# Two plain gate/up pairs a layer instead of four, with norm sums behind one begun product and FFN operands made name by name

## The chip, the cores and the metric

The kernel runs on one core of one Trainium2 chip. Times are device microseconds of one execution. The three runs of the kernel before took 1186.43, 1184.93 and 1186.91 us; the median, 1186.43 us, is the number that the change is measured against.

## The reference, cut to what matters

A trunk of two decoder layers over 512 tokens of width 1024, in float32. Layer 0 mixes tokens by three groups of dilated window attention, layer 1 by causal trailing means. Behind each mixer stands a SwiGLU feed-forward network (FFN) with 2816 hidden channels, and every part begins with an RMS norm.

```python
def rmsnorm(x, g):
    y = xf * lax.rsqrt(jnp.mean(xf * xf, axis=-1, keepdims=True) + RMS_EPS)
    return (y * g.astype(jnp.float32)).astype(x.dtype)
...
def swiglu_ffn(h, w_gate_up, w_down):
    gu = h @ w_gate_up
    gate, up = gu[..., :D_FF], gu[..., D_FF:]
    return (jax.nn.silu(gate) * up) @ w_down
...
    for i in range(DEPTH):
        ...
        x = x + swiglu_ffn(rmsnorm(x, ffn_norm[i]), w_ffn_gate_up[i], w_ffn_down[i])
    return rmsnorm(x, final_norm)
```

## The kernel before, in words

Channels lie on the 128 partitions and the 512 tokens along the free axis, so x is eight tiles `X[k]` of 128x512. For precision every operand is split into a high and a low part (`split`, line 91: ScalarE rounds the high part, VectorE subtracts it to get the low part), and each logical matmul is three: high by high, high by low, low by high (lines 329 to 332 and 461 to 463).

**Two ways to multiply.** A *plain* product (class `Product`) contracts all eight channel tiles: 24 matmuls of 512 columns. It can begin on x scaled by the norm's weights alone, before the row of 1/rms is known, since that row multiplies the result per token and is applied by VectorE afterwards (`plain_pair`, line 1093: `gt` and `up` are the product times `row`). A *Strassen pair* (`chained`, line 519) makes two output tiles, gate and up, by seven block products of 12 matmuls with 256 columns each, 84 in all, in place of 48 with 512. Its operands are seven combinations of blocks of the normed x (named "11", "1", "2", "21", "3", "22", "4"), kept in the dict `T` for the whole layer, and they need the finished row. `prepare(k)` (line 1108) makes all names for one channel tile `k`. In `chained` most block products accumulate onto one PSUM tile `alpha` one after another, and between two of them ScalarE copies what stands there so far (`a`, `b`, `c`; lines 535, 543 and 551).

**The FFN** (`ffn`, line 1086). There are 22 gate/up pairs j. The first `NPLAIN` = 4 are plain: their matmuls keep TensorE going while VectorE and ScalarE prepare `T`, one tile after each gate product. The others are Strassen pairs. `PARTS` splits the down projection into four parts: hidden tiles 0 to 1 (plain), 2 to 9 and 10 to 17 (block products), 18 to 21 (plain). The down projection of a part is called FF2 here, so FF2 part 1 is the plain one over the first two hidden tiles; it stands between gate/up pair 3 and pair 4.

**The norm in between.** Each finished `X[k]` is scaled and split (`note`, line 397) and squared on ScalarE, and VectorE adds the squares up in `acc`. `finish` (line 436) sums over channels by small matmuls with a tile of ones (`rstd`, line 411), VectorE scales (`var`, line 414), POOL raises to -1/2 (line 417), TensorE spreads the result over partitions (line 424) and ScalarE copies it to `row` (line 430). To cover that, `begin` starts two plain products ahead of the sums on the tiles that are there already, and a third one stands half ahead of the spread and half behind it.

**What sets the order.** Weights go through rings of buffers (`w` has five, `raw` four); `pump` issues loads and one conversion step after another between products, in the order of the list of weights. A plain tile's low part is made "lean": ScalarE writes minus the high part and a DMA of POOL's queue adds the source to it (line 149). A Strassen pair's weights (`Pair`) are three loads by SP and one adding DMA of POOL (line 173); one of its `raw` tiles is then combined by VectorE (lines 189 and 190), and its tiles are split by ScalarE and VectorE. The list of instructions that each engine then works through, strictly in order, is set when the program is built.

Of the kernel before, what the change touches and what calls it, by code (L numbers as in the profile page):

```python
# [15 lines left out]
P = 128  # L16
S = 512
# [21 lines left out]
K2 = KC // 2  # L39
NPLAIN = 4  # L40
WARM = 5
# [8 lines left out]
APART = 28  # L50
NEAR = 11
OPEN = 2
FIXED = NEAR + OPEN
# [12 lines left out]
def trunk(ctx: ExitStack, tc: tile.TileContext, xT, xN, norms, w_first, w_qk, w_qkp, w_v0, w_v0p, w_v12, w_out, w_outp, w_pair, w_down, w_dblock, w_pin, w_pgrp,  # L66
# [134 lines left out]

    turn = [0]
# [176 lines left out]

    def square(layer, k, engine=None):  # L380
        sq = tmp.tile([P, S], F32, name="sq", bufs=3)
        nc.scalar.activation(sq, X[k], AF.Square)
        if layer in acc:
            (engine or nc.vector).tensor_add(sq, acc[layer], sq)
        acc[layer] = sq

    def scaled(layer, k, hi, lo, on_dve=False):
# [7 lines left out]
        operand[layer, k] = hi, lo  # L395

    def note(layer, k):

        if layer < 4:
            held[layer, k], t = slot("h", open=layer == 2 and k == KC - 1)  # L400
            scaled(layer, k, t[:, 0], t[:, 1])
        square(layer, k)
# [197 lines left out]
    with tc.tile_pool(name="opool", bufs=1) as opool:  # L600
        early = [opool.tile([P, 2, S], F32R, tag=f"o{k}", name="early") for k in range(K2)]
        with tc.tile_pool(name="apool", bufs=1) as apool:
# [285 lines left out]
            def halve(h):  # L888

                if h < 3:  # L890
                    OP2[h] = tuple(apool.tile([P, S], F32R, tag=f"qk{h}{c}", name="oh") for c in range(2))
                else:
                    held["o", h], b = slot("oh", open=h == 3)
                    OP2[h] = b[:, 0], b[:, 1]
# [156 lines left out]

            def residual(m, p):
                x = X[m].rearrange("p (q c r) -> p q c r", c=NT, r=NT)
                nc.vector.tensor_add(x, x, p.rearrange("p (r c q) -> p q c r", r=NT, c=NT))
                note(1, m)

            for m in range(NOUT):
                residual(m, lead.pop(0).add([last]).p)
            for u in range(2):
                one, two = (apool.tile([P, S], F32, tag=tag, name="one") for tag in ("s0", "s12"))  # L1060
                seven(T2, one, two, scratch)
                if u:
                    for k in range(2):
                        give(("s", k))
                for c, p in enumerate((one, two)):
                    residual(NOUT + 2 * u + c, p)
            f = Product(HEADS, heads).add(range(HEADS))
            for key in [key for key in held if key[0] == "o"]:
                give(key)
            residual(KC - 1, f.p)  # L1070

    with tc.tile_pool(name="fpool", bufs=2) as fpool:
# [13 lines left out]
        def ffn(layer, nxt, lead, row):  # L1086
# [3 lines left out]
            def gu():  # L1090
                return lead.pop(0).p if lead else product(op)

            def plain_pair(j, up):
                pg = gu()
                gt = ftile("gt")
                nc.vector.tensor_mul(gt, pg, row)
                prepare(j)
                pu = gu()
                if j == NPLAIN - 1:
                    for k in range(KC):  # L1100
                        give((op, k))
                nc.vector.tensor_mul(up, pu, row)
                nc.scalar.activation(gt, gt, AF.Silu)
                nc.vector.tensor_mul(up, up, gt)

            T = {}

            def prepare(k):


                h, t = normed(op, k, row, Temp(), Temp(), True)
                hq, b22 = h.t.rearrange("p (a b c) -> p a b c", a=2, b=2), h.t[:, 3 * H2:]
                held["t", k, 0], b = slot("tb", apart=True)
                split(b[:, 0].rearrange("p (a c) -> p a c", a=2), b[:, 1].rearrange("p (a c) -> p a c", a=2), hq[:, :, 0])
                T["11", k], T["21", k] = (tuple(b[:, e, i * H2:(i + 1) * H2] for e in range(2)) for i in range(2))
                for i, names in enumerate((("1", "2"), ("3", "4"))):
                    held["t", k, 1 + i], b = slot("tt", apart=True)
                    split(b[:, 0], b[:, 1], t.t[:, i * S:(i + 1) * S])
                    for a, name in enumerate(names):
                        T[name, k] = tuple(b[:, e, a * H2:(a + 1) * H2] for e in range(2))  # L1120
                if k % 2 == 0:
                    held["t", k, 3], T["n"] = slot("tn", apart=True)
                n = tuple(T["n"][:, e, k % 2 * H2:(k % 2 + 1) * H2] for e in range(2))
                split_neg(*n, b22)
                T["22", k] = n
                h.done()
                t.done()

# [45 lines left out]
            def strassen_pair(u, first=None, right=None):  # L1174
# [10 lines left out]
                if first:  # L1185
                    hooks.setdefault(2, []).extend([later(give, ("t", k, 1)) for k in range(K2)] + [first])
                if right:
# [8 lines left out]
            def gate_up(j, ahead):  # L1196
                first, block = next((p[0], p[2]) for p in PARTS if p[0] <= j < p[1])
                u = tmp.tile([P, S], F32, tag="sq", name="u", bufs=3) if block or ahead else ftile("up")
                i, odd = (j - first) // 2, j % 2
                if j < NPLAIN:  # L1200
                    plain_pair(j, u)
                elif block and odd and j == FC - 1:
                    strassen_pair(u, later(operands, i, U["even"]), later(operands_right, i, u))
# [23 lines left out]

            j = 0
            for first, end, block in PARTS:
                while j < min(max(end + block, NPLAIN), FC):  # L1230
                    gate_up(j, block and j == end)
# [30 lines left out]

        lead = begin(2, 1, range(KC - 1))
        row = finish(lead, 1, [KC - 1])
        ffn(0, 2, lead, row)
# [11 lines left out]
        lead = begin(2, 2, range(KC - 2))  # L1277
        row = finish(lead, 2, range(KC - 2, KC))
        Y = {}
# [38 lines left out]
        def mix(g):  # L1318
            if g not in M:
                mixed(g)  # L1320
            for c, f in enumerate(M.pop(g)):
                m = 2 * g + c
                nc.vector.scalar_tensor_tensor(X[m], f.p, nrm[:, 5, m:m + 1], X[m],
                                               op0=OP.mult, op1=OP.add)
                held[3, m], t = slot("n")
                scaled(3, m, t[:, 0], t[:, 1])
            for c in range(2):
                square(3, 2 * g + c)
                give(("y", g, c))

        pool(3)
# [195 lines left out]
```

## Time and profile before

| | us |
|---|---|
| median of three runs | 1186.43 |
| the profiled execution: from the first to the last instruction (its span) | 1184.0 |
| ScalarE (ACT) busy | 721.7 |
| GpSimd (POOL) busy | 171.3 |

The difference between span and time, 2.4 us to the median, lies ahead of the first and behind the last instruction. In the rows of the profile PE is TensorE, DVE is VectorE, ACT is ScalarE; L461 is line 461; `ps<-far,w` names the tile written and the tiles read. A timeline row gives start, duration, engine, line, operation, tiles, shape and, in brackets, how long the engine sat idle before it and what ended that. A row of the windows view gives, for one stretch of time, the busy time of PE, PE's weight loads, DVE, ACT and POOL (with the number of instructions), then the granted clock, the DMA engines' busy share and GB/s. A row of the waits list gives the time waited in all, how often, and the longest wait.

### The profile page before, as it was taken

Reading aid. Unit: us, or ns where it says so; the run is one execution under the profiler, and the core shown is the slowest. Engines: PE = TensorE matmul, PEld = TensorE weight load, DVE = VectorE, ACT = ScalarE, POOL = GpSimd, SP = SyncE. Lnnn points to the kernel's source line nnn. Section 1 sums busy time; section 2 is a strip of 40 time slices with the busy share of each in tenths; the row PEclk is TensorE's granted clock in tenths of the full one; section 3 lists DMA queues with packets and bytes.
Section 4 is the critical chain, followed back from the end, with each engine's and each line's share of the span. In section 5 each row is a group of like instructions: output and inputs, shape, how many; then the busy total and the mean of one; then the engine's idle time right before and its main releaser. Section 6 shows DMA issues by size and latency. Waiting matters only on the chain.

```text
span 1184.0 us, 25180 instructions
## 1 busy us (share of the span) xinstructions
PE 1175.4 (99%) x10042; PEld 1119.9 (95%) x10042; DVE 989.0 (84%) x1733; ACT 721.7 (61%) x1262; POOL 171.3 (14%) x165
## 2 busy tenths in 40 slices
PE   9999999999999999999999999999999999999997
PEld 7889999999999989889999999988889999999997
DVE  7997898889789888699988988656789998898875
ACT  6554564546455557747756775775575766676553
POOL 1101111111111002311111111122130111111100
PEclk9999999999999999999999999999999999999999
DMA  8537667666856557957777877798595777877732
GB/s 302 130 95 187 147 153 166 168 160 152 192 140 169 145 157 195 246 113 203 191 188 189 204 184 209 195 265 208 121 195 119 187 199 195 198 191 193 197 92 72
DMA packets 83766, 207.57 MB, mean 175 GB/s; under 512 B 7856, under 2 KB 13120, under 8 KB 83648
## 3 DMA queue, kind: packets, MB, share of 16 engines
q1 hardware_dynamic: 52672, 144.84, 36.9%
q0 software_dynamic: 30688, 60.83, 31.6%
q8 instruction: 78, 1.28, 0.4%
q14 instruction: 40, 0.33, 0.1%
q10 hardware_dynamic: 288, 0.29, 0.1%
HBM read 203.84 MB, written 2.10 MB: 174 GB/s over the span
## 4 chain that ended last, share of the span: by engine, by line
PE 96%; DMA 1%; issue 1%; DVE 1%; ACT 0%; POOL 0%; POOLq 0%; DVEq 0%; ACTq 0%
PE ps L461 21%; PE ps L462 20%; PE ps L463 20%; PE ps L329 7%; PE ps L330 7%; PE ps L332 7%; PE ps L928 2%; PE ps L632 2%; PE ps L633 2%; PE ps L634 2%; DMA raw<-w_outp 1%; PE ps L847 1%; PE ps L716 1%; PE ps L736 1%; PE ps L841 1%
## 5 line engine op out<-in xcount | busy, mean ns | idle before, releaser
L92 ACT ACTIVATE w<-raw 128x1024 fp32r<-128x1024 f32 x268 | 283.7, 1063 | 177.0 <-PE ps L463 73.3
L93 DVE TENSOR_TENSOR w<-raw,w 128x1024 fp32r<-128x1024 f32 x268 | 326.4, 1222 | 48.8 <-ACT w L92 44.7
L461 PE MATMUL ps<-far,w 128*128 128x256 f32 x896 | 246.5, 275 | 0.0
L462 PE MATMUL ps<-far,w 128*128 128x256 f32 x896 | 246.4, 275 | 0.0
L463 PE MATMUL ps<-far,w 128*128 128x256 f32 x896 | 246.4, 275 | 0.0
L461 PE MATMUL ps<-near,w 128*128 128x256 f32 x676 | 190.5, 282 | 0.0
L462 PE MATMUL ps<-near,w 128*128 128x256 f32 x676 | 186.9, 277 | 0.0
L463 PE MATMUL ps<-near,w 128*128 128x256 f32 x676 | 186.9, 276 | 0.0
L462 PEld LDWEIGHTS ps<-far,w 128*128 128x128 f32 x896 | 168.2, 188 | 0.1
L461 PEld LDWEIGHTS ps<-far,w 128*128 128x128 f32 x896 | 168.2, 188 | 0.1
L463 PEld LDWEIGHTS ps<-far,w 128*128 128x128 f32 x896 | 168.2, 188 | 0.0
L461 PEld LDWEIGHTS ps<-near,w 128*128 128x128 f32 x676 | 127.1, 188 | 0.5
L462 PEld LDWEIGHTS ps<-near,w 128*128 128x128 f32 x676 | 127.1, 188 | 0.0
L463 PEld LDWEIGHTS ps<-near,w 128*128 128x128 f32 x676 | 127.0, 188 | 0.0
L329 PE MATMUL ps<-near,w 128*128 128x512 f32 (+1 forms) x316 | 119.4, 379 | 0.0
L332 PE MATMUL ps<-near,w 128*128 128x512 f32 (+1 forms) x316 | 118.7, 376 | 0.0
L330 PE MATMUL ps<-near,w 128*128 128x512 f32 (+1 forms) x316 | 118.7, 376 | 0.0
L173 POOL DMA_DIRECT2D raw<-w_pair x36 | 43.6, 1210 | 291.7 <-DMA raw<-w_pair 87.3
L329 PEld LDWEIGHTS ps<-near,w 128*128 128x128 f32 x316 | 59.3, 188 | 11.0 <-ACT near L92 0.4
L332 PEld LDWEIGHTS ps<-near,w 128*128 128x128 f32 x316 | 59.3, 188 | 10.9
L330 PEld LDWEIGHTS ps<-near,w 128*128 128x128 f32 x316 | 59.4, 188 | 10.6 <-DVE near L93 0.2
L92 ACT ACTIVATE half<-rawhalf 128x512 fp32r<-128x512 f32 x84 | 52.8, 630 | 13.7 <-PE ps L463 11.8
(333 smaller groups left out, 2802.7 us busy)
## 6 DMA issues: line engine op xcount, KB each, us to landing
raw<-w_pair SPq DMA_DIRECT2D x80, 512.0 KB, 4.9
raw<-w_qkp SPq DMA_DIRECT2D x38, 512.0 KB, 4.5
raw<-w_pair POOLq DMA_DIRECT2D x36, 512.0 KB, 7.6
raw<-w_dblock SPq DMA_DIRECT2D x32, 512.0 KB, 4.7
raw<-w_qkp POOLq DMA_DIRECT2D x19, 512.0 KB, 7.5
raw<-w_v SPq DMA_DIRECT2D x18, 512.0 KB, 4.1
rawhalf<-w_pair SPq DMA_DIRECT2D x36, 256.0 KB, 5.2
raw<-w_dblock POOLq DMA_DIRECT2D x16, 512.0 KB, 7.5
```

Of the source, the lines that this page charges most:

```text
L92: nc.scalar.activation(hi, v, AF.Copy)
L93: nc.vector.tensor_tensor(lo, v, hi.bitcast(F32), op=OP.subtract)
L173: nc.gpsimd.dma_start(self.b.rearrange("p (a c) -> p a c", a=2), self.src[:, None, 3 * n:].to_broadcast([P, 2, n]), accum_op=OP.add)
L329: nc.tensor.matmul(self.p[:, cols], w[0][:, s], mh[:, cols], start=self.done == 0, stop=False)
L330: nc.tensor.matmul(self.p[:, cols], w[0][:, s], ml[:, cols], start=False, stop=False)
L332: nc.tensor.matmul(self.p[:, cols], w[1][:, s], mh[:, cols], start=False, stop=self.done == self.n)
L461: nc.tensor.matmul(dst, w.t[0][:, c], th, start=k == 0 and not on, stop=False, skip_group_check=on)
L462: nc.tensor.matmul(dst, w.t[0][:, c], tl, start=False, stop=False, skip_group_check=on)
L463: nc.tensor.matmul(dst, w.t[1][:, c], th, start=False, stop=k == n - 1, skip_group_check=on)
L632: nc.tensor.matmul(o, mh, wh, start=k == 0, stop=False)
L633: nc.tensor.matmul(o, mh, wl, start=False, stop=False)
L634: nc.tensor.matmul(o, ml, wh, start=False, stop=k == K2 - 1)
```

## The change

Four things change, all around the beginning of an FFN:

1. `NPLAIN` goes from 4 to 2: pairs 2 and 3 of each layer become Strassen pairs.
2. `prepare(k)` goes; a generator `prepared` makes the operands name by name for all channel tiles, in the order in which the block products read them, and yields between groups.
3. FF2 part 1 now stands behind pair 2 (the first Strassen pair) and ahead of pair 3.
4. `finish` takes lists: what is added to begun products ahead of the sums (`now`), between sums and spread (`behind`), and after it (`rest`). In layer 0 one product is begun on seven tiles and a second is begun only behind the sums. A flag `hold` keeps `pump` from making weights in the last steps of layer 0's mixer, and there the squares are summed before the tiles are scaled and split. In layer 1 likewise tile 0 and 1 are squared first.

The numbers `NEAR` and `OPEN` only move two operand slots from one tile to tiles of their own.

```diff
-NPLAIN = 4
+NPLAIN = 2
...
-            if not steps or not free(steps[0][1]):
+            if not steps or not free(steps[0][1]) or (hold[0] and not must):
...
-    def finish(lead, layer, ks):
+    def finish(lead, layer, now, behind, rest=()):
 
-        for f in lead:
+        for f, ks in now:
             f.add(ks)
         r = rstd([acc[layer]])
-        lead += begin(1, layer, range(4))
+        for f, ks in behind:
+            f.add(ks)
+        if not behind:
+            lead += begin(1, layer, range(4))
+            rest = [(lead[-1], range(4, KC))]
         row = row_of(spread(r))
-        lead[-1].add(range(4, KC))
+        hold[0] = False
+        for f, ks in rest:
+            f.add(ks)
         return row
...
-            residual(KC - 1, f.p)
+            noted(1, KC - 3)
+            summed_up(1, squared(KC - 3))
+            noted(1, KC - 2)
+            sq = squared(KC - 2)
+            grown(KC - 1, f.p)
+            summed_up(1, sq)
+            summed_up(1, squared(KC - 1))
+            noted(1, KC - 1)
...
+                normed(0)
+                each(lambda p: named("11", p, a(p, 0)))
+                each(lambda p: nc.vector.tensor_sub(a(p, 0), a(p, 1), a(p, 0)))
+                each(lambda p: named("1", p, a(p, 0)))
+                yield
+                normed(1)
+                each(lambda p: nc.vector.tensor_sub(a(p, 0), a(p, 0), d(p, 1)))
+                each(lambda p: named("2", p, a(p, 0)))
+                yield
+                each(lambda p: named("21", p, d(p, 0)))
+                each(lambda p: nc.vector.tensor_sub(a(p, 1), d(p, 1), a(p, 1)))
+                each(lambda p: named("3", p, a(p, 1)))
+                yield
+                each(lambda p: named("22", p, d(p, 1), split_neg))
+                each(lambda p: nc.vector.scalar_tensor_tensor(d(p, 0), a(p, 0), -1.0, d(p, 0), op0=OP.mult, op1=OP.subtract))
+                each(lambda p: named("4", p, d(p, 0)))
...
+            stage, ready = prepared(T), []
+            for i in range(4):
+                next(stage)
+                if i % 2 == 0:
+                    while len(lead) + 2 * len(ready) < 2 * NPLAIN - 1 + i // 2:
+                        lead.extend(begin(1, op, range(KC)))
+                elif i == 1:
+                    ready.append(scaled_pair(0))
...
+            for j in range(1, NPLAIN):
+                ready.append(scaled_pair(j))
+            for j, (gt, up) in enumerate(ready):
+                gated(gt, up)
...
-                while j < min(max(end + block, NPLAIN), FC):
+                while j < min(max(end + (block or not first), NPLAIN), FC):
...
-        lead = begin(2, 1, range(KC - 1))
-        row = finish(lead, 1, [KC - 1])
+        lead = begin(1, 1, range(KC - 1))
+        lead.append(Product(KC, stream(1)))
+        row = finish(lead, 1, [], [(lead[1], range(4))], [(lead[0], [KC - 1]), (lead[1], range(4, KC))])
...
-        for f in lead:
-            f.add(range(2, 4))
-        row = finish(lead, 3, range(2))
+        row = finish(lead, 3, [(f, range(2, 4)) for f in lead], [(lead[0], range(2)), (lead[1], range(1))], [(lead[1], range(1, 2))])
```

How this moves the instructions is seen at two places of layer 0; layer 1 looks the same there but for what is said in the prediction.

ScalarE's list before, around the first Strassen pair of layer 0 (pair 4; `w` and `raw` are weights, `ps_6520` is that pair's `alpha`, `first` and `sums` hold the copies of it and of the second sum):

```order
L92 ACTIVATE w_6479<-raw_6304 128x1024
L92 ACTIVATE near_82<-t_6599 128x256 x2
L92 ACTIVATE w_6514<-raw_6305 128x1024
L535 COPY first_6523<-ps_6520 128x256
L539 COPY sums_6524<-ps_6522 128x256
L92 ACTIVATE near_82<-u_6274 128x256 x2
L543 COPY first_6523<-ps_6520 128x256
```

And after the change, around its first Strassen pair (pair 2, whose `alpha` is `ps_6301`; `temp` are the normed combinations, `far` the finished operands, `gt_6288` the gate of plain pair 1, `up_6228` and `up_6289` the gated products of pairs 0 and 1):

```order
L92 ACTIVATE far_6069<-temp_6171 128x512
L92 ACTIVATE w_6358<-raw_6160 128x1024
L92 ACTIVATE far_6069<-temp_6172 128x512
L92 ACTIVATE far_6069<-temp_6173 128x512
L1127 ACTIVATE gt_6288<-gt_6288 128x512
L551 COPY first_6304<-ps_6301 128x256
L555 COPY sums_6305<-ps_6303 128x256
L92 ACTIVATE near_82<-up_6228 128x512
L92 ACTIVATE near_82<-up_6289 128x512
L559 COPY first_6304<-ps_6301 128x256
```

Before, all operands of the pair were made long ahead, and parts of the next hidden tiles stand between the copies. Now the last operand parts (of "4"), the silu of plain pair 1 and the split of a weight tile of the next Strassen pair, into the ring buffer that block product "21" frees, stand ahead of the first copy, and the two gated products ahead of the next copy of `ps_6301`. On TensorE the pair's products follow in the order "11", "1", "21", "2", the beginning of "22", "3", the rest of "22", "4"; "11", "2", "3" and "4" go to `ps_6301`.

VectorE's list before, from the last residual of layer 0's mixer to the first use of the row (`x_5535` is the last tile of x, `sq` the squares and their sums):

```order
L1054 TENSOR_TENSOR x_5535<-x_5535,ps_6029 128x512
L394 SCALAR_TENSOR_TENSOR near_82<-x_5535,nrm_75,near_82 128x512
L384 TENSOR_TENSOR sq_6063<-sq_6026,sq_6063 128x512
L414 TENSOR_SCALAR var_6150<-ps_6133 128x4
L1096 TENSOR_TENSOR gt_6200<-ps_6072,row_6173 128x512
```

And after the change (`x_5537` is the last tile; `raw_5949`, `raw_5950` and `w_6137` belong to the first Strassen pair's weights):

```order
L1070 TENSOR_TENSOR x_5537<-x_5537,ps_6023 128x512
L400 SCALAR_TENSOR_TENSOR near_82<-x_5535,nrm_75,near_82 128x512
L93 TENSOR_TENSOR w_6137<-raw_5949,w_6137 128x1024
L387 TENSOR_TENSOR sq_6059<-sq_6055,sq_6059 128x512
L400 SCALAR_TENSOR_TENSOR near_82<-x_5537,nrm_75,near_82 128x512
L189 TENSOR_TENSOR raw_5949<-raw_5949,raw_5950 128x512
L190 TENSOR_TENSOR raw_5949<-raw_5949 128x512
L424 TENSOR_SCALAR var_6110<-ps_6093 128x4
L1143 SCALAR_TENSOR_TENSOR temp_6170<-x_5530,nrm_75,row_6132 128x512
```

A weight split now stands ahead of the last sum of squares, and the two combinations of the Strassen pair's raw weights between that sum and `var`. The 33 instructions of VectorE from the last row shown to the one that writes `gt_6288` (line 1126) make the operands "11" to "3" and part of "4", and scale plain pair 0.

More of the change, by code (lines that the diff above doesn't have):

```diff
@@ L1090, in gu, with scaled_pair @@
             def gu():
[L1091 to L1102, printed above, removed]
+                return lead.pop(0).p
+            def scaled_pair(j):
+                gt, up = ftile("gt"), (tmp.tile([P, S], F32, tag="sq", name="u", bufs=3) if j > 1 else ftile("up"))
+                for t in (gt, up):
+                    nc.vector.tensor_mul(t, gu(), row)
@@ L1103, in plain_pair, with gated @@
                 nc.scalar.activation(gt, gt, AF.Silu)
+                return gt, up
+            def gated(gt, up):
                 nc.vector.tensor_mul(up, up, gt)
             T = {}
[L1108 to L1127, printed above, removed]
@@ L1185, in strassen_pair @@
                 if first:
[L1186 removed]
+                    hooks.setdefault(2, []).extend([later(give, ("t", name, p)) for name in "12" for p in range(2)] + [first])
                 if right:
@@ L1277, in trunk @@
         lead = begin(2, 2, range(KC - 2))
-        row = finish(lead, 2, range(KC - 2, KC))
+        row = finish(lead, 2, [(f, range(KC - 2, KC)) for f in lead], [])
         Y = {}
@@ L1329, in mix @@
                 give(("y", g, c))
+            for c in range(2):
+                if not g:
+                    held[3, c], t = slot("n")
+                    scaled(3, c, t[:, 0], t[:, 1])
         pool(3)
```

74 lines of the change are left out of this document (57 added, 17 removed).

## The prediction

> **What bounds the kernel now.** I read the page's busy times and clock first, then TensorE's waits, then the timeline at the places that the change touches.
>
> ```profile
> span 1184.0 us, 25180 instructions
> PE 1175.4 (99%) x10042; PEld 1119.9 (95%) x10042; DVE 989.0 (84%) x1733; ACT 721.7 (61%) x1262; POOL 171.3 (14%) x165
> PEclk9999999999999999999999999999999999999999
> ```
> ```profile
> PE ps L908 <- DVE idle L905: 1.2, 1, 1.2
> PE ps L841 <- ACT t L808: 0.8, 1, 0.8
> ```
> TensorE is busy for 99% of the span at full clock, and its waits list holds two entries, 2.0 us in all. So a matmul taken out shortens the run by its issue interval, and each wait that the change gives TensorE lengthens it by its whole length. VectorE is 84% busy over the span, and full in places. The span of the profiled execution is 1184.0 us; the median shown is 1186.43, 2.4 us more. I sum against the span and carry the difference over to the median.
>
> **TensorE's own work.**
> ```profile
> 500.00 0.39 PE L332 MATMUL ps<-near,w 128*128 128x512 f32 x1
> 500.22 0.39 PE L329 MATMUL ps<-near,w 128*128 128x512 f32 x1
> 529.84 0.28 PE L461 MATMUL ps<-far,w 128*128 128x256 f32 x1
> 529.96 0.28 PE L462 MATMUL ps<-far,w 128*128 128x256 f32 x1
> ```
> Matmuls overlap, so what counts is start to start: about 0.227 us at 512 columns, 0.1133 at 256 (168 of them stand between 522.66 and 541.70 in the timeline). A plain pair is 48 matmuls of 512, 10.9 us; a Strassen pair is 84 of 256, 9.5 us. Four pairs change kind: 4 x 1.38 = **5.5 us saved**. Nothing else is added to TensorE: the order has exactly 4 x 36 = 144 matmuls more.
>
> **What lies between the norm row and the first Strassen pair.** Before, half a plain product, five whole ones and FF2 part 1 lie there: 180 matmuls, about 40 us. Now the pair follows after two products. The rows around the row of norms, layer 0:
>
> ```profile
> 480.94 1.05 PE L424 MATMUL ps<-ident,rcol 128*128 128x128 f32 x8
> 481.75 0.48 PE L329 MATMUL ps<-near,w 128*128 128x512 f32 x1
> 482.03 0.60 ACT L430 ACTIVATE row<-ps 128x512 f32<-128x512 f32 x1 [0.98 <-PE ps L424]
> 482.66 0.69 DVE L1096 TENSOR_TENSOR gt<-ps,row 128x512 f32<-128x512 f32 x1 [4.27 <-ACT row L430]
> ```
> Call S the start of the first matmul behind the spread (481.75): VectorE starts at S + 0.9. From S, TensorE now has 15 matmuls of the begun products, 48 of the next two, and three block products of 12: 63 x 0.227 + 36 x 0.1133 = 18.4 us. The fourth block product ("2") accumulates onto the PSUM tile of the first, which ScalarE's copy (`first`, line 551 after the change) must have read. That copy stands behind the silu of the second plain pair, and the silu needs VectorE's `gt_6288`. From the row to `gt_6288` VectorE has 33 instructions: 12 scalar_tensor_tensor and 19 tensor_tensor of 512 columns, 2 weight splits of 1024.
>
> ```profile
> 502.54 1.22 DVE L93 TENSOR_TENSOR w<-raw,w 128x1024 fp32r<-128x1024 f32 x1
> 503.67 0.68 DVE L93 TENSOR_TENSOR far<-temp,far 128x512 fp32r<-128x512 f32 x1
> 505.54 0.74 DVE L578 SCALAR_TENSOR_TENSOR temp<-x,nrm,row 128x512 f32<-128x512 f32 x1
> 506.21 0.68 DVE L189 TENSOR_TENSOR raw<-raw 128x512 f32<-128x512 f32 x1
> 506.81 0.68 DVE L1096 TENSOR_TENSOR gt<-ps,row 128x512 f32<-128x512 f32 x1
> ```
> Start to start these are 1.13, 0.67 and 0.60 us, on an engine that never rests there. The sum is 12 x 0.67 + 19 x 0.60 + 2 x 1.13 = 21.7. So `gt_6288` is there at S + 0.9 + 21.7 + 0.1 = S + 22.7.
>
> ```profile
> 485.26 1.05 ACT L146 ACTIVATE w<-raw 128x1024 fp32r<-128x1024 f32 x1
> 486.21 0.62 ACT L92 ACTIVATE far<-temp 128x512 fp32r<-128x512 f32 x1
> 489.03 0.62 ACT L92 ACTIVATE near<-up 128x512 fp32r<-128x512 f32 x1
> 489.55 0.61 ACT L1103 ACTIVATE gt<-gt 128x512 f32<-128x512 f32 x1
> 524.26 0.37 ACT L535 COPY first<-ps 128x256 f32<-128x256 f32 x1 [0.29 <-PE ps L463]
> ```
> The silu takes 0.6 and the copy 0.37: TensorE goes on at about S + 23.7 where it stood at S + 18.4, **a wait of 5.3 us in layer 0**. Bounds: not under 2.9, even with VectorE far ahead, since ScalarE's split of the next `w` (0.95) can begin only when the third block product has left its buffer, and two operand parts and the silu (0.52 each, start to start) and the copy follow; not over 7, with a us of VectorE waiting for ScalarE.
>
> Next, product "3" overwrites the same tile and needs the second copy (line 559), behind ScalarE's two `near<-up` parts. Those wait for five instructions of VectorE behind `gt_6288` (two parts of `4`, `up`, two gatings): the first starts at S + 22.6, the last 4 x 0.60 later, and 0.7, 0.52 and 0.37 follow: S + 26.6, where TensorE is ready 16 matmuls of 256 later, at S + 25.5. **Another 1.1 us** (0 to 2).
>
> **Layer 1** has 51 matmuls of 512 between spread and pair, not 63, since 3 instead of 15 remain of the begun products.
> ```profile
> 863.39 0.48 PE L329 MATMUL ps<-near,w 128*128 128x512 f32 x1
> 864.30 0.69 DVE L1096 TENSOR_TENSOR gt<-ps,row 128x512 f32<-128x512 f32 x1 [4.20 <-ACT row L430]
> ```
> The same 0.9 us. TensorE: 51 x 0.227 + 4.1 = 15.7. VectorE: one split fewer, 20.6, so `gt` is there at S + 21.5, and silu and copy end at S + 22.5. **6.8 us** (5.5 to 8). Of these 0.9 fall inside the third product, whose "21" parts VectorE finishes only at about S + 15.3 and 15.9; the rest is the copy's. Then 1.1 for product "3" again.
>
> **The norm sum of layer 0.** The product before it starts at 461.28; TensorE then has 24 + 48 matmuls up to the sums, now 24 + 21.
> ```profile
> 461.28 0.40 PE L329 MATMUL ps<-oh,w 128*128 128x512 f32 x1
> 477.71 0.43 PE L411 MATMUL ps<-ones,sq 128*32 128x1 f32 x32
> 478.23 0.16 DVE L414 TENSOR_SCALAR var<-ps 128x4 f32<-128x4 f32 x1 [4.80 <-PE ps L411]
> 478.47 1.39 POOL L417 TENSOR_TENSOR rcol<-var,nhalf 128x2 f32<-128x2 f32 x2 [5.08 <-DVE var L414]
> ```
> ```profile
> raw<-w_pair SPq DMA_DIRECT2D x2, 512.0 KB, 11.1
> w<-w_pair POOLq DMA_DIRECT2D x2, 512.0 KB, 9.7
> ```
> TensorE reaches them at 461.28 + 45 x 0.227 = 471.5, and the spread, 12 matmuls behind, at 474.6. The reordered squares should be summed near 472, so that costs about 0.7. But `var` now stands on VectorE behind the addition `raw_5949 += raw_5950`, whose operand is first loaded, then added to by a DMA of POOL's queue. Those two rows are the DMAs issued between 455 and 470: 11.1 and 9.7 us to land. Issued near 456 (the loads of this place go out from 455.3 on), the load lands near 466, POOL's near 475.5; then two additions, `var`, 1.39 on POOL: spread at about 478.1 instead of 474.6. **3.5 us** (0.7 if the data are early, 5 by both landings in full). POOL's queue holds behind that DMA the additions for the second plain pair's weights; they land near 477 to 479 and are first read near S + 3.5, which hides them; if not, each us is a us. In layer 1 the loads go out a pooling stage ahead, and 8 matmuls of cover (1.8 us) stand against `var` and POOL's 1.39: 0.2 us (0 to 1.5).
>
> **The clock.**
> ```profile
> 1180.00:1182.00 2.00, 0.00 (x0) 0.00 (x0) 0.00 (x0) 0.00 (x0) 0.00 (x0) 1.00 1.02 384
> 1182.00:1184.00 2.00, 0.00 (x0) 0.00 (x0) 0.00 (x0) 0.00 (x0) 0.00 (x0) 0.52 0.07 23
> 1176.77 0.88 PE L1397 MATMUL ps<-ident,ends 128*128 128x128 f32 x6
> ```
> TensorE's last matmul ends at 1177.65, and the granted clock (the column before the DMA share) has gone to about half a little after 1182.0: 4.4 us of idleness cost the clock. Waits of 5.3 and 5.9 us are longer. At half clock the fourth product takes 1.36 us more and the four matmuls behind it 0.45; the wait for the second copy hides 1.1 of that. I take **0.7 us a layer** (0, if the clock holds, to 2.5, if it stays low for several us; how long that lasts no row shows). [...]
>
> **Sum.** -5.5 + layer 0 (5.3 + 1.1 + 3.5) + layer 1 (6.8 + 1.1 + 0.2) + clock 1.4 = +13.9: span 1197.9, median 1186.43 + 13.9 = **1200 us**. FF2 part 1 behind the first pair costs nothing more: its operands are split some 3 us before TensorE gets there (S + 27.2 against S + 30.3), and its 48 matmuls (10.9 us) let VectorE's 8 additions and 3 splits (8.2) through. SP issues as many DMAs as before.
>
> **Rivals.**
> - *The fourth product doesn't wait for the copy.* If TensorE accumulates onto a tile that is still being read, the 13.4 us of waits for the copies and the clock's 1.4 go, and 1185.5 is left: not slower. It decides wherever the copy isn't what the product waits for. For it: before, no product ever waited there. Against: before, ScalarE sat idle 0.29 us until the product was there (524.26), so the copy could not be late. With the norm sum on time as well it is 1182. Chance 0.09.
> - *VectorE is ahead*, because much of its list runs faster than these rows: only ScalarE's 2.9 a layer stay, without the clock: -5.5 + 2 x (2.9 + 1.1) + 0.9 + 3.7 = +7.1, so 1193.5, or 1190 with the data on time. Against: the rows' rate held for 20 us on end. Chance 0.11.
> - *Late weights.* The loads before the first pair meet queues that are full (11.1 us to land); 3 to 6 us more: 1203 to 1206. Chance 0.08.
> - *The clock stays low longer* after both waits: 2 x 1.8 more, 1204. Chance 0.10.
> - The forecast: 0.62, on its own 1195 to 1204.
>
> **How the numbers follow.** The range 1190 to 1206 takes in all but the first rival and the far ends. A difference under 0.2% (2.4 us) can't be told from none. Faster 0.04, same 0.06, slower 0.90.
>
> **What would show it.** In the new profile TensorE's waits list should have the L551 copy in both layers at 5 to 6 us, the L559 copy at about 1, a wait for the spread in layer 0, and VectorE without a gap from the row to the second `gt`. If that copy isn't in the list, the main step is wrong; if the wait is there but near 3 us, VectorE's rate is; if the clock row stays at 9 throughout, the clock term is.

## The result, and the profile after

The changed kernel takes **1199.83 us** (median of 4, 1199.05 to 1201.8) where the kernel before takes 1186.67 (median of 4 beside it): a ratio of 1.0118, 95% interval 1.0104 to 1.0132. That is 13.2 us slower, and 1200.0 was predicted.

The page of the changed kernel: span, busy times, and the clock granted to TensorE in 40 slices.

```profile
span 1200.0 us, 25505 instructions
PE 1177.6 (98%) x10186; PEld 1128.4 (94%) x10186; DVE 1008.3 (84%) x1753; ACT 725.5 (60%) x1274; POOL 166.5 (14%) x157
PEclk9999999999999999899999999999989999999999
```

144 matmuls more, as forecast, and two slices in which the clock is not full. They are the places of the first Strassen pair of each layer. The two profiled executions are 16.0 us apart (1184.0 and 1200.0), more than the medians: the one of after was the slowest of its four, 2.0 us above the median.

TensorE's list of waits (what waited, for what: us in total, times, longest):

```profile
PE ps L477 <- ACT first L551: 10.1, 2, 5.4
PE ps L434 <- POOL rcol L427: 2.5, 1, 2.5
PE ps L924 <- DVE idle L921: 1.2, 1, 1.2
PE ps L857 <- ACT t L824: 1.2, 1, 1.2
PE ps L478 <- DVE far L93: 0.6, 1, 0.6
```

The third and fourth row stood in the list of before too (1.2 and 0.8 there). New are the first copy (line 551) in both layers, the spread in layer 0, and in layer 1 the short wait for the "21" parts. The second copy (line 559) isn't in the list.

Layer 0 in the timeline: start and length in us, engine, line, and in brackets the idle time before and who ended it. 479.63 is S, the first matmul behind the spread.

```profile
479.63 0.47 PE L329 MATMUL ps<-near,w 128*128 128x512 f32 x1
480.54 0.75 DVE L1143 SCALAR_TENSOR_TENSOR temp<-x,nrm,row 128x512 f32<-128x512 f32 x1 [2.91 <-ACT row L440]
498.04 0.28 PE L479 MATMUL ps<-far,w 128*128 128x256 f32 x1
501.39 0.68 DVE L1126 TENSOR_TENSOR gt<-ps,row 128x512 f32<-128x512 f32 x1
502.11 0.63 ACT L1127 ACTIVATE gt<-gt 128x512 f32<-128x512 f32 x1
502.64 0.35 ACT L551 COPY first<-ps 128x256 f32<-128x256 f32 x1
503.05 0.58 PE L477 MATMUL ps<-far,w 128*128 128x256 f32 x1 [4.73 <-ACT first L551]
506.01 0.38 ACT L559 COPY first<-ps 128x256 f32<-128x256 f32 x1 [0.27 <-PE ps L479]
```

VectorE starts at S + 0.9, TensorE could go on from the third block product 0.11 us after 498.04, at S + 18.5, and gt is made by S + 22.4. The silu and the copy follow it at once, and TensorE goes on at S + 23.4. The last row answers for the second copy: it was ScalarE that waited for TensorE there, 0.27 us, not the other way round.

The clock over that place, in stretches of 2 us (stretch, its length, TensorE busy and its matmuls, granted clock, DMA share, GB/s):

```profile
498.00:500.00 2.00, 0.32 (x3) 1.00 1.00 176
500.00:502.00 2.00, 0.00 (x0) 0.84 0.87 169
502.00:504.00 2.00, 0.95 (x4) 0.50 1.08 188
504.00:506.00 2.00, 2.00 (x12) 0.50 1.23 197
506.00:508.00 2.00, 2.00 (x11) 0.50 0.42 69
508.00:510.00 2.00, 2.00 (x18) 0.95 0.00 0
```

The clock falls to half at 501.38, 3.1 us after TensorE's last matmul ended (498.32), and stays there for 5.2 us after TensorE has gone on, to 508.21: the matmuls of 256 columns then start every 0.213 us, not every 0.113. In layer 1 it is the same, and longer (887.1 to 897.3).

The norm sum of layer 0:

```profile
467.50 1.20 POOL L173 DMA_DIRECT2D raw<-w_pair  x1 [4.76 <-DMA raw<-w_pair]
472.61 0.43 PE L421 MATMUL ps<-ones,sq 128*32 128x1 f32 x32
476.15 0.69 DVE L189 TENSOR_TENSOR raw<-raw 128x512 f32<-128x512 f32 x1 [3.02 <-issue]
476.88 0.69 DVE L190 TENSOR_TENSOR raw<-raw 128x512 f32<-128x512 f32 x1
477.48 0.15 DVE L424 TENSOR_SCALAR var<-ps 128x4 f32<-128x4 f32 x1
478.50 1.38 PE L434 MATMUL ps<-ident,rcol 128*128 128x128 f32 x8 [2.51 <-POOL rcol L427]
```

The sums were ready at 473.04. VectorE stood idle for 3.02 us at the first of the two weight additions, until the DMA that POOL had issued at 467.50 into the same weights landed at 476.07, 0.08 us ahead of its start. var takes 0.15 us and had to stand behind both additions.

### The profile page after: what moved, and what is told of

Read it like the earlier page. It is cut to its first block, busy times and chain, and to the rows that moved or that the text cites. A ratio compares the mean times of both kernels' runs of the same rounds, so it can differ in the third digit from the quotient of the medians.

```text
span 1200.0 us, 25505 instructions
## 1 busy us (share of the span) xinstructions
PE 1177.6 (98%) x10186; PEld 1128.4 (94%) x10186; DVE 1008.3 (84%) x1753; ACT 725.5 (60%) x1274; POOL 166.5 (14%) x157
## 4 chain that ended last, share of the span: by engine, by line
PE 89%; DVE 5%; DMA 2%; issue 2%; ACT 1%; POOL 1%; POOLq 0%; DVEq 0%; SPq 0%; ACTq 0%
PE ps L477 21%; PE ps L479 21%; PE ps L478 21%; PE ps L329 5%; PE ps L330 5%; PE ps L332 5%; PE ps L944 2%; PE ps L648 2%; PE ps L650 2%; PE ps L649 2%; DMA raw<-w_outp 1%; PE ps L863 1%; DVE far L93 1%; PE ps L732 1%; DMA raw<-w_pair 1%
## 5 line engine op out<-in xcount | busy, mean ns | idle before, releaser
L92 ACT ACTIVATE w<-raw 128x1024 fp32r<-128x1024 f32 x280 | 296.2, 1063 | 175.2 <-PE ps L479 77.0
L93 DVE TENSOR_TENSOR w<-raw,w 128x1024 fp32r<-128x1024 f32 x280 | 340.9, 1221 | 53.1 <-ACT w L92 48.8
L477 PE MATMUL ps<-far,w 128*128 128x256 f32 x992 | 275.5, 278 | 10.1 <-ACT first L551 10.1
L478 PE MATMUL ps<-far,w 128*128 128x256 f32 x992 | 275.3, 278 | 0.6 <-DVE far L93 0.6
L479 PE MATMUL ps<-far,w 128*128 128x256 f32 x992 | 275.1, 277 | 0.0
L477 PEld LDWEIGHTS ps<-far,w 128*128 128x128 f32 x992 | 188.6, 190 | 10.7 <-ACT first L551 10.5
L478 PEld LDWEIGHTS ps<-far,w 128*128 128x128 f32 x992 | 188.8, 190 | 1.0 <-DVE far L93 0.8
L479 PEld LDWEIGHTS ps<-far,w 128*128 128x128 f32 x992 | 188.6, 190 | 0.0
L477 PE MATMUL ps<-near,w 128*128 128x256 f32 x558 | 157.9, 283 | 0.0
L478 PE MATMUL ps<-near,w 128*128 128x256 f32 x558 | 154.3, 277 | 0.0
L479 PE MATMUL ps<-near,w 128*128 128x256 f32 x558 | 154.2, 276 | 0.0
L477 PEld LDWEIGHTS ps<-near,w 128*128 128x128 f32 x558 | 104.9, 188 | 0.5
L478 PEld LDWEIGHTS ps<-near,w 128*128 128x128 f32 x558 | 105.0, 188 | 0.0
L479 PEld LDWEIGHTS ps<-near,w 128*128 128x128 f32 x558 | 104.9, 188 | 0.0
L173 POOL DMA_DIRECT2D raw<-w_pair x40 | 48.4, 1210 | 340.7 <-DMA raw<-w_pair 159.7
L329 PE MATMUL ps<-near,w 128*128 128x512 f32 (+1 forms) x232 | 86.5, 374 | 0.0
L330 PE MATMUL ps<-near,w 128*128 128x512 f32 (+1 forms) x232 | 86.1, 371 | 0.0
L332 PE MATMUL ps<-near,w 128*128 128x512 f32 (+1 forms) x232 | 86.0, 371 | 0.0
L189 DVE TENSOR_TENSOR raw<-raw 128x512 f32<-128x512 f32 x88 | 60.1, 683 | 4.6 <-issue 4.2
L190 DVE TENSOR_TENSOR raw<-raw 128x512 f32<-128x512 f32 x88 | 60.0, 682 | 0.2
L93 DVE TENSOR_TENSOR half<-rawhalf,half 128x512 fp32r<-128x512 f32 x88 | 60.0, 682 | 0.0
```

The lines of the kernel that those rows point to most:

```text
L92: nc.scalar.activation(hi, v, AF.Copy)
L93: nc.vector.tensor_tensor(lo, v, hi.bitcast(F32), op=OP.subtract)
L173: nc.gpsimd.dma_start(self.b.rearrange("p (a c) -> p a c", a=2), self.src[:, None, 3 * n:].to_broadcast([P, 2, n]), accum_op=OP.add)
L189: nc.vector.tensor_add(a[:, :n], a[:, :n], b[:, :n])
L190: nc.vector.tensor_add(a[:, n:], a[:, n:], a[:, :n])
L329: nc.tensor.matmul(self.p[:, cols], w[0][:, s], mh[:, cols], start=self.done == 0, stop=False)
```

## The experiments

The account to be tested: the first Strassen pair of each layer now comes before VectorE's list behind the norm row is done, TensorE waits for a copy that stands behind that list in ScalarE's queue, and the wait costs the clock as well. Its rivals: that the operands made name by name, or the norm sums behind one product, are dear in themselves, and that the clock costs nothing. Each kernel is compared with the kernel before on the same chip (whose medians there were 1186.4, 1185.9 and 1186.3).

| kernel | median us | ratio to before, 95% interval |
|---|---|---|
| the change | 1199.83 | 1.0118 (1.0104 to 1.0132) |
| norm_old | 1201.34 | 1.0126 (1.0112 to 1.0139) |
| gt_first | 1191.52 | 1.0045 (1.0033 to 1.0058) |
| warm (30 matmuls) | 1198.95 | 1.0106 (1.0092 to 1.0119) |
| warm40 | 1196.87 | 1.0091 (1.0077 to 1.0105) |
| n3 | 1190.94 | 1.0042 (1.0028 to 1.0056) |
| n4 | 1186.28 | 1.0002 (0.9993 to 1.0011) |
| var_act | 1197.58 | 1.0097 (1.0081 to 1.0112) |
| gt_var | 1189.42 | 1.0024 (1.0015 to 1.0033) |
| ff2_first | 1227.37 | 1.0346 (1.033 to 1.0362) |

**Which part of the change costs: n4.**

```diff
-NPLAIN = 2
+NPLAIN = 4
...
-                    while len(lead) + 2 * len(ready) < 2 * NPLAIN - 1 + i // 2:
+                    while len(lead) + 2 * len(ready) < 2 * min(NPLAIN, 3) - 1 + i // 2:
...
             for j in range(1, NPLAIN):
+                if j == 3:
+                    lead.extend(begin(2, op, range(KC)))
                 ready.append(scaled_pair(j))
...
-                else:
+                elif j == 2:
                     U["even"] = up
+                else:
+                    late.extend([later(operands, 0, U["even"]), later(operands_right, 0, up), later(operands_left, 0, up)])
```

> The changed kernel with four plain pairs a layer, as before, and FF2 part 1 right behind them; the norm sums and the operands made name by name stay as changed. Theory 1 (the fewer plain pairs alone open the waits, since 40 us of matmuls cover VectorE's list again; the norm sums cost what stands ahead of them in the queues, 0 to 2 us): 1186.5 to 1188.5, and no wait for a copy. Rival 2 (the operands made name by name are dear in themselves): 1192 or more. Rival 3 (the norm sums behind one product bring something): under 1185.

1186.28, the time of before to within 0.1%, and 0.2 us under the range that was given. Its whole list of waits is a row that stands in every kernel:

```profile
PE ps L924 <- DVE idle L921: 1.2, 1, 1.2
```

So the operands made name by name and the norm sums behind one product cost nothing and bring nothing while four plain pairs stand there. What costs is that two of them are gone.

**How much cover is enough: n3.**

```diff
-NPLAIN = 2
+NPLAIN = 3
...
-            while j < min(max(end + (block or not first), NPLAIN), FC):
+            while j < min(max(end + (block or 2 * (not first)), NPLAIN), FC):
```

> The changed kernel with three plain pairs a layer instead of two, and FF2 part 1 again behind the first Strassen pair after them. TensorE has 2 x 1.38 = 2.8 us more work than in the changed kernel, but 10.9 us more cover ahead of the first Strassen pair. Theory 1: the waits for the copy (4.9, and 0.8 + 5.4) and the loss of clock go but for 0.5 to 2 us in all: 1186 to 1188, the time of before to within 0.2%. Rival (the waits come from the operands made name by name, whatever stands ahead): the waits stay, 1197 or more.

1190.94: outside what was expected. The copies went as forecast, but the spread did not. From its waits, and POOL's timeline there:

```profile
PE ps L434 <- POOL rcol L427: 2.0, 1, 2.0
PE ps L477 <- ACT first L559: 0.5, 1, 0.5
```
```profile
471.13 1.23 POOL L173 DMA_DIRECT2D raw<-w_pair  x1 [8.29 <-DMA rawhalf<-w_pair]
471.85 2.34 POOL L149 DMA_DIRECT2D w<-w_pair  x2
474.10 2.96 POOL L427 TENSOR_TENSOR rcol<-var,nhalf 128x2 f32<-128x2 f32 x2
```

The waits for copies are down from 10.1 us to 0.5. Now var is ready at 471.8 (it started at 471.60 and took 0.17), and its power stands on POOL behind a DMA issue that had waited 8.29 us for a landing, and behind the issues that had piled up after that one. The same wait of 2 us, from another queue, and here it cost the clock as well (the windows have the columns of the clock table above):

```profile
476.00:478.00 2.00, 1.56 (x9) 0.68 1.13 199
478.00:480.00 2.00, 2.00 (x7) 0.50 1.14 208
```

The clock was at half for 3.4 us from 476.72 on, while TensorE worked: 1.7 us more, so the spread cost 3.8 us with its wait of 2.1 start to start, where the expectation had 0.5 to 2 us for all that was left. Taken off, it would leave this execution 1184.6 us, under the 1186.4 of before: an estimate, and from one execution. It does not explain all of the 3 to 5 us above the expectation: the profiled execution was the fastest of five (1188.4; the slowest 1192.5). Three of the other four have its mean clock (0.997) and the slowest 0.996, so more time at half clock explains little of what they lost; the rest isn't shown.

**Is it the place in the queue: gt_first.** No work added or removed, only the order in which the second plain pair's scaling and the last names are written:

```diff
                     while len(lead) + 2 * len(ready) < 2 * NPLAIN - 1 + i // 2:
                         lead.extend(begin(1, op, range(KC)))
+                    if i == 2:
+                        ready.append(scaled_pair(1))
...
-            for j in range(1, NPLAIN):
+            for j in range(2, NPLAIN):
                 ready.append(scaled_pair(j))
```

> The changed kernel with one line moved: the second plain pair's gt and up are made ahead of the last stage of the names (22 and 4), not behind it. No work is added or taken away. Theory 1 (the first copy is late because it stands behind the silu of the second gt, which VectorE makes as its 33rd instruction): gt becomes its 27th, 3.7 us earlier, and two operand parts and a weight split leave ScalarE's queue ahead of the copy; the waits for the first copy fall from 4.9 to 1 or 2 us in layer 0 and from 5.4 to about 3 in layer 1, too short for the clock to fall: 1189 to 1192. Rival (the copies are late for another reason, the weights or VectorE's whole list, or what is gained here is waited for again at FF2 part 1): 1196 or more.

1191.52, as expected: 8 of the 13 us come back by a move. Waits, and ScalarE at the copy in layer 0:

```profile
PE ps L477 <- ACT first L551: 4.2, 2, 2.6
```
```profile
496.57 1.13 ACT L92 ACTIVATE far<-temp 128x512 fp32r<-128x512 f32 x2
497.61 0.61 ACT L1127 ACTIVATE gt<-gt 128x512 f32<-128x512 f32 x1
498.13 0.35 ACT L551 COPY first<-ps 128x256 f32<-128x256 f32 x1
498.65 1.07 ACT L92 ACTIVATE w<-raw 128x1024 fp32r<-128x1024 f32 x1
```

The silu is earlier, the copy is still right behind it, and the weight split that stood ahead is behind. In layer 0 the clock held behind a wait of 1.6 us (4.2 less 2.6); in layer 1 a wait of 2.6 us behind the short one for "21" (0.6) still cost 3.4 us at half clock. That 3 us would be too short for the clock to fall was an assumption of the expectation, which no run had shown. Nothing that was gained was lost again at FF2 part 1.

**Do the parts add up: norm_old.**

```diff
-        lead = begin(1, 1, range(KC - 1))
-        lead.append(Product(KC, stream(1)))
-        row = finish(lead, 1, [], [(lead[1], range(4))], [(lead[0], [KC - 1]), (lead[1], range(4, KC))])
+        lead = begin(2, 1, range(KC - 1))
+        row = finish(lead, 1, [(f, [KC - 1]) for f in lead], [])
```

> The changed kernel with the norm sums of layer 0 put back behind two products that have begun. Theory 1 (the copy's queue on ScalarE sets the wait, and what TensorE has between the spread and the first Strassen pair is its cover): the 2.5 us wait for the spread goes, but 27 matmuls of 512 columns (6.1 us) move from behind the spread to ahead of it, while VectorE loses only two weight splits (2.3 us) from its list up to the second gt. So TensorE's waits inside the first pair of layer 0 grow by about 4 us, to 9 in all: 1201 (1199 to 1203), no better than the changed kernel. Rival 2 (the parts of the change add up, each with its own price): 2.5 to 2.9 us gained, 1197.

1201.34, as the account has it. The row of the spread is gone from the list, and another has grown:

```profile
PE ps L477 <- ACT first L551: 11.0, 3, 5.4
PE ps L478 <- DVE far L93: 3.5, 2, 2.9
```

Beside the copy's, layer 0 has a wait of 2.9 us inside the third block product: with 36 matmuls of 512 behind the spread instead of 63, TensorE overtakes VectorE sooner. So the earlier norm sums move cover from ahead of the row to behind it, and taking them back saves nothing in all, though their wait of 2.5 us goes. Whether they gain anything isn't shown: 1201.34 and 1199.83 are 1.5 us apart, and the intervals of the two ratios overlap.

**What the clock costs: warm and warm40.** Unread matmuls fill the wait:

```diff
         mult(beta, wb, 1, T, "21", n)
         wb.done()
+        if spare:
+            pz = ps()
+            for i in range(spare):
+                nc.tensor.matmul(pz[:, :H2], ws.t[0][:, :P], T["21", n - 1][0], start=True, stop=True)
```

> The changed kernel with 30 matmuls of 256 columns (3.4 us), whose result nothing reads, between the third and the fourth block product of the first Strassen pair of each layer. They fill the wait; the copy comes no earlier. Theory 1: the two waits shrink to 1.5 and 2 us and end when they did, the clock stays at 1.00, and the 2.4 and 3.0 us that the matmuls behind the waits lost at half clock come back; of them the wait for product 3's copy, which the half clock hid, takes 0.6 in each layer: 1195.6 (1194.5 to 1197). Rival 2 (the loss behind the waits is the second copy's, or VectorE's, and not the clock's): 1199 to 1200. Rival 3 (the added matmuls delay the pair): 1201 or more.

1198.95: less was gained than expected, and by the time alone rival 2 (1199 to 1200) would do as well. In layer 0 the wait for the copy was 1.5 us and the clock held. In layer 1 the wait was 2.7 us, and the clock fell all the same (889.5 to 892.9). The expectation had taken a wait of 2 us there. And in layer 0 the clock fell at another place, where it had held in the changed kernel: behind the spread, after a wait of 2.3 us by the list (476.5 to 479.9):

```profile
476.00:478.00 2.00, 1.28 (x6) 0.62 1.07 204
478.00:480.00 2.00, 2.00 (x8) 0.52 0.46 84
```

TensorE worked for 3.2 and 3.4 us of the two falls, so they cost some 1.6 and 1.7 us: about as much as the time lies above the 1195.6 of theory 1. So the second try:

> The kernel with unread matmuls in the wait, now 40 of 256 columns instead of 30 (4.5 us). With 30 the wait of layer 1 was still 2.7 us, and the clock fell there; in layer 0 it was 1.5 us, and the clock held. Theory 1 (the clock's fall is a price of its own): both waits are now under 1.6 us, the clock holds at 1.00 in both layers, and 1.2 us come off the run with 30: 0.9987 of it, some 1197.7; the waits still end where they did. Rival (the added matmuls delay the pair by themselves, or the half clock cost nothing): the time stays or grows by up to 1.1 us a layer.

1196.87. Its waits for the two copies, and the clock in layer 1:

```profile
PE ps L478 <- ACT first L552: 1.6, 2, 1.4
PE ps L478 <- ACT first L560: 0.5, 2, 0.3
```
```profile
886.00:888.00 2.00, 0.60 (x6) 1.00 1.04 176
888.00:890.00 2.00, 2.00 (x16) 1.00 1.22 197
890.00:892.00 2.00, 1.73 (x15) 1.00 0.34 52
```

The clock is full throughout (0.999 in the mean), behind the spread too, and the kernel is 3 us faster than the change with 80 matmuls more in it. Up to 1.3 of these 3 us are the spread's and not the clock's, since its wait is 1.2 us in this profile and 2.5 in the changed kernel's. And with the clock full the second copy (line 560 here) is waited for after all, 0.2 to 0.3 us a time by the list; it stands behind one split of `up` here, where it stands behind two in layer 0 of the changed kernel. So the fall of the clock is a price of its own, and it hid the second copy.

**Is the spread's wait a place in VectorE's order: var_act.**

```diff
-        nc.vector.tensor_scalar(v, pc[:, :nt], 1.0 / D, EPS, op0=OP.mult, op1=OP.add)
+        if on_act:
+            nc.scalar.activation(v, pc[:, :nt], AF.Copy, scale=1.0 / D, bias=EPS)
+        else:
+            nc.vector.tensor_scalar(v, pc[:, :nt], 1.0 / D, EPS, op0=OP.mult, op1=OP.add)
```

> The changed kernel with one small instruction moved to another engine: in layer 0 the scaling of the norm sums (var, 128x4) is done by ScalarE, not by VectorE, where it stands behind two additions that wait for a landing. Theory 1 (the wait for the spread is that place in VectorE's order): the 2.5 us wait for the spread goes. VectorE, which still waits for the landing, then starts its list about 0.9 us later behind the row, so the wait for the first copy in layer 0 grows by that: net -1.7, 1198 (1197 to 1199). Rival 2 (the price is 2.5 us whole): 1197. Rival 3 (POOL's queue or the squares are late, and VectorE's order isn't the cause): no change, 1199.8.

1197.58.

```profile
473.05 0.17 ACT L425 ACTIVATE var<-ps 128x4 f32<-128x4 f32 x1 [2.34 <-PE ps L421]
474.94 0.69 DVE L189 TENSOR_TENSOR raw<-raw 128x512 f32<-128x512 f32 x1 [2.45 <-issue]
475.76 1.05 PE L437 MATMUL ps<-ident,rcol 128*128 128x128 f32 x8
```

VectorE still stands idle for its landing; var no longer does, and the spread follows the matmuls ahead without idling. Theories 1 and 2 lie 1 us apart, and the time lies between them. The profile is for the second: the landing came early enough here (VectorE went on at 474.94, before the row) that its list was not pushed back, and the wait for the copy stayed at 4.7 us.

**Both moves: gt_var.** The diffs of gt_first and var_act together.

> Both moves at once: the second gt ahead of the last stage of the names, and var of layer 0 on ScalarE. Theory 1: the wait for the spread (2.4 us in the run with the first move alone) goes, VectorE starts its list about 0.9 us later behind the row, so the first copy's wait in layer 0 grows from 1.8 to about 2.7 us; that may cost the clock one stretch of 3.4 us at half rate (1.2 us): 1189.7 (1188.5 to 1191). Still slower than before by some 0.3%, since the waits of layer 1 (0.8 and 2.6 us) stay and the Strassen pairs give only 5.5. Rival (with VectorE's list shorter the plain pairs are no longer needed, and the change brings its 5.5 us): 1184 or less.

1189.42, as expected, though by another way in layer 0: the wait stayed at 1.8 us and the clock held there. What stays is the copy's wait in both layers (the longer one, 2.6 us, in layer 1) and the short one for the "21" parts in layer 1:

```profile
PE ps L480 <- ACT first L554: 4.2, 2, 2.6
PE ps L481 <- DVE far L93: 0.6, 1, 0.6
```

It is the best version found with two plain pairs, and still 0.24% slower than before.

**FF2 part 1: ff2_first and ff2_again.** In both loops that plan and run the pairs:

```diff
-            while j < min(max(end + (block or not first), NPLAIN), FC):
+            while j < min(max(end + block, NPLAIN), FC):
```

> The changed kernel with FF2 part 1 put back ahead of the first Strassen pair, still with two plain pairs. FF2 part 1 reads what the plain pairs give, and that is split last on VectorE's list, some 26 us behind the row; TensorE is there after 63 and 51 matmuls of 512 (14.3 and 11.6 us). Theory 1 (VectorE's list decides, whatever TensorE does next): waits of about 13 and 16 us take the place of the copy's, the pair behind them waits for nothing, and with the clock's loss it is 1212 to 1224. Rival (the place of FF2 part 1 doesn't matter, or it covers the copy): 1200 or less.

> The kernel with FF2 part 1 ahead of the first Strassen pair once more, for its waits: the profiled execution of the first try was disturbed (4213 us, TensorE slowed throughout), and its time of 1227 is 3 us above what was expected. Theory 1: TensorE waits for the near parts of up (ScalarE's split of the plain pairs' outputs) ahead of FF2 part 1, 13 to 16 us in layer 0 and 16 to 18 in layer 1, and runs at half clock for one to three stretches of 3.4 us behind each; no wait for a copy. Rival: a third wait, for weights that come late because the queues stand still, explains the rest.

1227.37, and 1227.19 in a second run, above the range that was given.

```profile
PE ps L329 <- ACT near L92: 29.3, 2, 16.6
PE ps L434 <- POOL rcol L427: 8.6, 1, 8.6
```

The two waits ahead of FF2 part 1 are as forecast (29.3 in all), and the rival is right that there is a third wait: the spread waits 8.6 us, since POOL's timeline has a DMA issue waiting 10.56 us for a landing ahead of the power, and one more that went out only at 481.60 (what released that one isn't shown). The clock fell behind this wait as well, for 10.2 us. So this edit of the change is needed: with two plain pairs it is worth some 27 us.

## Why the prediction was right, point by point

- **Fewer matmul columns, -5.5.** The losses listed here sum to 19.8 us, and the span grew by 16.0; with -5.5 that leaves 1.7 us elsewhere, 0.4 of them in the wait for `t` (1.2 for 0.8). Right to within that.
- **First copy, layer 0, 5.3.** 4.9 start to start. TensorE at S + 18.5 (18.4 forecast), copy over at S + 23.4 (23.7). VectorE's list, the step on which it rested, took 0.3 us less than its 22.7. gt_first shows that it is the place on the list that decides.
- **First copy, layer 1, 6.8.** 6.4, of them 0.8 inside the third product (0.9 forecast).
- **Second copy, 1.1 a layer.** Failed in this kernel: nobody waited for it. The step took TensorE at full rate behind the wait; at half rate product "2" took so long that the copy waited for it. warm40, at full rate, has 0.2 to 0.3 us a layer in a slightly other order.
- **Norm sum of layer 0, 3.5.** 2.7 start to start; var behind the additions, and the additions behind a landing, as the step had it (var_act). Layer 1's 0.2 did not appear.
- **The clock, 0.7 a layer.** Mis-sized, the largest error of the sum: 2.4 us in layer 0 and 2.9 in layer 1 (24 and 29 matmuls at 0.213 us instead of 0.113), and 0.3 us more for the first matmul behind each wait. The step took the half rate to end with the next few matmuls; it lasted 5.2 and 6.2 us after TensorE had gone on. This is what the fourth rival supposed, with a chance of 0.10 and a price of 3.6 us above the forecast; no row or run shows its 1.8 us a layer, and 4.4 us in all above the forecast was measured.
- **The sum.** The clock took 4.4 us more than forecast; the second copy 2.2, the norm sums 1.0, and the first copies 0.8 less. +13.9 was forecast, 13.2 separates the medians. The place, the order and the main size were right; that the total is so close is partly errors that cancel.
- **The other rivals.** That TensorE wouldn't wait for the copy: it did, 4.73 and 5.39 us. That VectorE would be ahead: it was 0.3 us ahead of the forecast, not 2.4. Late weights in the first pair: no such wait in the list; where landings did count (the spread) it was through another engine's queue.

No version here beats the kernel before. The Strassen pairs bring 5.5 us, and with two plain pairs the waits left in layer 1 alone, with the clock's share, cost about as much. Left open: whether var's power on another engine than POOL would let n3 through, which wasn't tried, and why n3's executions differ by 4 us at nearly the same mean clock.

## What to carry to other kernels

Ask of a product that goes away what it covered: count the instructions on the other engines between the last common point and the first result that is needed, and set their time against the matmuls left over that stretch: here 22.4 us from S to `gt` against 18.5. The copy that frees the accumulator takes 0.35 us here, and TensorE waited 4.73 us for it, since it stood behind a silu that had to wait for VectorE. So write what TensorE waits for ahead of what it doesn't; one moved statement gave back 8 of 13 us. And before an early reduction is bought, look at what stands on its engine waiting for a landing: it was VectorE in the changed kernel (3.02 us) and POOL in n3 (8.29 us).

## What the hardware showed unexpectedly

The half-rate stretches of these runs come in steps of one length. The waits are start to start; the time at half clock is taken from stretches of 0.5 us, as the sum of the clock that was missing, doubled:

| kernel, layer | wait ahead, us | at half clock, us |
|---|---|---|
| the change, 0 | 4.9 | 6.83 |
| the change, 1 | 0.8 and 5.5 | 10.24 |
| var_act, 0 | 4.9 | 3.41 |
| var_act, 1 | 0.8 and 5.6 | 6.83 |
| gt_first, 1 | 0.8 and 2.7 | 3.41 |
| gt_var, 1 | 0.8 and 2.7 | 6.82 |
| warm, 1 | 2.7 | 3.42 |
| warm, 0, the spread | 2.4 | 3.41 |
| n3, 0, the spread | 2.1 | 3.42 |
| norm_old, 0 | 3.1 and 5.6 | 10.24 |
| norm_old, 1 | 0.8 and 5.6 | 10.24 |
| ff2_again, 0 and 1 | 12.9 and 16.7 | 13.66 and 20.48 |
| ff2_again, 0, the spread | 8.8 | 10.24 |

All are multiples of 3.413 us (a sixth of the longest, 20.48) to within 0.02. The falls of the two layers are whole numbers of such steps apart too: 385.70 us in the changed kernel (501.38 and 887.08) and in var_act (500.58 and 886.28), which is 113.0 steps, and 389.12 us in norm_old (496.34 and 885.46), which is 114.0. So a wait had no fixed price here: the same 4.9 us cost two steps in the changed kernel and one in var_act. Two cases with the same wait differ in the work in the first step: in gt_first, layer 1, TensorE worked 3.1 of the 3.4 us (from 881.87, where its wait ended), and there was one step; in gt_var it worked 2.8 us (from 878.62), and there were two.

TensorE was not idle for the whole of every step that ends with a fall. In the one that ends at 887.08 in the changed kernel it was busy for 1.55 of the 3.41 us, and in norm_old, layer 0, for some 1.5, where the clock fell (496.34) as the second wait began. The spread's wait in the changed kernel, 2.5 us, lies across two steps as counted back from 501.38, with 1.92 and 2.40 us of work, and cost no clock; n3's shorter one, 2.0 us by the list, left 1.4 us of work in the step from 473.31 to its fall at 476.72, and cost it. Where a bound lies isn't shown: in var_act, layer 0, the clock held behind a step in which TensorE was busy for 1.50 us (493.75 to 497.16), and in norm_old, layer 1, it fell behind one of 1.65 us (882.04 to 885.46).
